# Eight of eleven chunks of a down-projection as Strassen's seven products, with the residual kept in HBM

## The chip, the core and the metric

The kernel runs on one core of one Trainium2 chip. The metric is the time of one execution on the device in microseconds (us), as the median of several runs.

## What is computed

One decoder layer for 512 prompt tokens and 8 sample tokens: norm, a mixed attention and recurrence block, an output projection with its residual, and a convolutional feed-forward block with its residual, all in float32. The change touches the end of it:

```python
D_MODEL, D_FF, CONV_W = 2048, 5632, 3
def conv_ffn(h, w_up, conv_w, conv_b, w_down, prefix):
    u = jnp.matmul(h, w_up)                      # 520 tokens x 11264
    ...                                          # causal depthwise convolution of width 3
    gate, val = jnp.split(c, 2, axis=-1)
    y = jnp.matmul(jax.nn.gelu(gate) * val, w_down)   # 520 x 5632 times 5632 x 2048
    return y, up[:, -(CONV_W - 1):]
...
x = x + jnp.matmul(mix, w_out)
y, conv_new = conv_ffn(rms_norm(x, norm2), w_up, conv_w, conv_b, w_down, conv_buf)
x = x + y                                        # then the final rmsnorm
```

## The kernel before

Activations lie transposed, features on the 128 partitions and all 520 tokens along the free axis; a matmul takes one half of them, 260 columns. To keep float32 precision each operand is split into a high part (hi, written by ACT) and the rest (lo, one subtraction on DVE). A product is then three matmuls: hi with hi, hi with lo, lo with hi. A matmul on unsplit float32 operands is one instruction ("raw" below), and takes longer.

The feed-forward part has 44 inner tiles of 128 for each of gate and value, in 11 chunks of four. Three stages follow each other on TensorE: the last part of W_out, the up-projection, the down-projection.

- **Up-projection.** It is cut into 44 "pairs", two output tiles each, numbered 0 to 43. Pair 0 is done as it is: eight raw units of eight matmuls (`first_units`), while ACT and DVE prepare the operands of the others. Pairs 1 to 43 are done by Strassen's method (`up_units`): the weights as 2 x 2 blocks (output tile n, inner parity i), the activations as 2 x 2 blocks B (inner parity, token half). Seven units take the place of eight, with the operands t1 to t4, b11, b21 and b22, made once from B and kept split, two "slots" of SBUF each. In the order in which they run, the units are 1 (b11), 4 (t4), 5 (t1), 6 (t2), 7 (t3), 2 (b21), 3 (b22). The weight sums s1 to s3 of the next pair and s2's second form (`sum1` to `sum4`) are four DVE operations a pair. The partial results leave PSUM through q1, q2 and q3 into u; unit 3 adds onto the PSUM bank from which c22 has read. In pairs 1 and 2, b11 is not split yet, and unit 1 is raw. `prep_b11` splits it in place in pair 2: ACT writes b11h, DVE the difference b11x into spare tiles, ACT b11l.
- **Convolution.** When a pair is done, a generator (`conv`) works through the convolution one step per unit, beside the next pair; at each second pair POOL stores the gated result to HBM (`ad`).
- **Down-projection.** `plain` goes over five groups of two chunks and the last chunk: eight inner tiles (four at the end) for two output tiles at a time, each product as three matmuls on two token halves. The chunks' activations come back from `ad` and are split (a0 to a10). The residual x2, which was stored to HBM (`x2d`) at the start of the up-projection, is loaded whole, 4 MB, and stays in SBUF; every result is added to it.

The code is recorded in the order in which it is written out: `units` is one list of units, and the loop at the end issues, for unit k, the weight split of unit k+2 (`prod`), its `pre` functions, its matmuls, its `post` function, and one `step` of each generator. Each engine works through its own queue in that order. Weights are loaded by SP (`load_r`, three tiles of 1 MB), activations by POOL.

```python
def split(view):
    hi = wp.tile([P, nk, P], F32R, tag="hi", name="hi", bufs=3)
    S.activation(hi, view, AF.Copy)
    lo = wp.tile([P, nk, P], F32R, tag="lo", name="lo", bufs=3)
    V.tensor_tensor(lo, view, hi.bitcast(F32), op=ALU.subtract)
```

Of the kernel before, what the change touches and what calls it, by code (L numbers as in the profile page):

```python
# [17 lines left out]
P = 128  # L18
# [50 lines left out]
def hybrid_step(ctx: ExitStack, tc: tile.TileContext, I: dict, C: dict, O: dict):  # L69
# [952 lines left out]

    xop, B = {}, {}
    R, SS, GT, UC = {}, {}, {}, {}
    pairs = [(c, o, part) for c in range(NCH) for o in (0, 2) for part in range(2)]

    def load_pair(p, n):
        c, o, part = pairs[p]  # L1030
# [21 lines left out]
    def conv(p, u):  # L1052
        c, o, part = pairs[p]
        n0 = 44 * part + 4 * c + o
        if c not in UC:
            UC[c] = fwork([P, 2, 10, 4], "uc", 2)
        G.tensor_copy(UC[c][:, part, :, o:o + 2].rearrange("p r j -> p j r"), u[:, :, T:UW])
        cv = cvtile()
        G.tensor_copy(cv[:, :, T:TT], spre[:, n0:n0 + 2])
        for j in range(2):  # L1060
            n = slice(n0 + j, n0 + j + 1)
            S.activation(cv[:, j, 0:T], u[:, j, 0:T], AF.Identity, scale=convc[:, 0, n], bias=convc[:, 3, n])  # L1062
        yield
        for j in range(2):
            n = slice(n0 + j, n0 + j + 1)
            for i, w in ((1, T), (2, TT)):
                V.scalar_tensor_tensor(cv[:, j, 0:w], u[:, j, i:i + w], convc[:, i, n], cv[:, j, 0:w],  # L1067
                                       op0=ALU.mult, op1=ALU.add)
# [5 lines left out]
        V.tensor_tensor(cv, GT[c, o], cv, op=ALU.mult)  # L1074
        nc.gpsimd.dma_start(ad[c][:, o:o + 2], cv)
# [14 lines left out]
        next(g)  # L1090
        bg.append(g)

    def first_units():

        bank, uu = {}, []

        def unit(i, n, t):
            def mm(un):
                if i == 0:
                    bank[n, t] = bankp(2 - 2 * n + t)  # L1100
                ps = bank[n, t][:, 0:HALF]
                for m in range(8):
                    PE.matmul(ps, A(0, n, i)[:, m], xg[i][t][:, m], start=i == 0 and m == 0,
                              stop=i == 1 and m == 7, skip_group_check=True)
                if i == 1:
                    if not uu:
                        uu.append(utile())
                        G.memset(uu[0][:, :, 0:2], 0.0)
                    V.tensor_tensor(uu[0][:, n, 2 + HALF * t:2 + HALF * (t + 1)], ps,
                                    rbc1[:, HALF * t:HALF * (t + 1)], op=ALU.mult)  # L1110

            return Unit(None, mm, (lambda: start_conv(0, uu[0])) if (i, n, t) == (1, 0, 1) else None)

        return [unit(i, n, t) for n in (1, 0) for i in range(2) for t in range(2)]

    def up_units(p):
        first = p == 1
        bank, st, uu = {}, {}, []

        def u():  # L1120
            if not uu:
                uu.append(utile())
                G.memset(uu[0][:, :, 0:2], 0.0)
            return uu[0]

        def out(j, t):
            return u()[:, j, 2 + HALF * t:2 + HALF * (t + 1)]
# [32 lines left out]
        def post6():  # L1160
            add("q2", "q1", 2)

        def c21():
            V.tensor_tensor(out(1, 0), st["q3"], ps(4), op=ALU.subtract)

        def c22():
            V.tensor_tensor(out(1, 1), st["q3"], ps(3), op=ALU.add)

        def post7():
            add("q3", "q2", 0)  # L1170
            c22()
            if not first:
                c21()

        def post2():
            S.copy(out(0, 0), ps(1))
# [78 lines left out]
    def prep0():  # L1255
        drain()
        for i in range(2):
            for t in range(2):
                nc.gpsimd.dma_start(x2d.rearrange("p (m i) c -> p i m c", i=2)[:, i, :, HALF * t:HALF * (t + 1)],
                                    x2b[i][t])  # L1260

    def prep_t1():
        norm2()
# [16 lines left out]
        diff(B["t"], B["t"], B[2, 1])  # L1280
        xop["t4"] = split_act(B["t"], 9, 12, "t4")

    def prep_b11():

        hi = slot(3, "b11h")
        S.activation(hi, B[1, 1], AF.Copy)
        halves = []
        for a in (0, 4):
            h = ff.tile([P, 4, HALF], F32R, tag="cv", name="b11x", bufs=3)
            V.tensor_tensor(h, B[1, 1][:, a:a + 4], hi[:, a:a + 4].bitcast(F32), op=ALU.subtract)  # L1290
            halves.append(h)
        lo = slot(13, "b11l")
        for a, h in zip((0, 4), halves):
            S.activation(lo[:, a:a + 4], h.bitcast(F32), AF.Copy)
        xop["b11"] = hi, lo
# [53 lines left out]
    ngroup = (NCH + 1) // 2  # L1349
# [172 lines left out]
```

## Time and profile before

| | us |
|---|---|
| median of 3 runs | 2321.49 (2321.19 to 2324.48) |
| the profiled execution's own time | 2320.68 |
| its span, first to last instruction | 2318.9 |
| TensorE busy / VectorE / ScalarE / GpSimd | 2277.2 / 1458.5 / 903.3 / 184.4 |
| up-projection, pairs 0 to 43 | 858 to 1781 |
| down-projection, chunks 0 to 7 | 1781 to 2150 |
| down-projection, chunks 8 to 10, final norm | 2150 to 2319 |

PE is TensorE's matmuls, PEld its weight loads, DVE VectorE, ACT ScalarE, POOL GpSimd, SP the engine that issues the weight loads. In the slices of the span a digit is the busy share in tenths; a busy PE is not a PE at its peak, since matmuls are pipelined. PEclk is the clock granted to TensorE. In a line's row stand the number of instructions, their busy time and mean, and behind the bar the idle time ahead of them with what ended it. In the timeline a row is start, duration, engine, line, operation, and in square brackets the idle time ahead of it with its releaser.

### The profile page before, as it was taken

What the parts mean: (1) busy time and instruction counts of PE and PEld (TensorE: products, weight loads), DVE (VectorE), ACT (ScalarE), POOL (GpSimd) and SP (SyncE); (2) the same over time, 40 slices, a digit from 0 to 9 for tenths busy, and PEclk for the clock granted to TensorE, in tenths of its full rate; (3) what the DMA queues carried; (4) which work ended last, traced back from release to release, by engine and by line L of the source; (5) the groups of instructions that cost most, each with busy time, mean ns of one, the idle gap of its engine ahead of it and who ended that gap; (6) DMA issues with size and microseconds to landing.
All of it is one profiled execution on the core that took longest, in us unless ns stands there. A gap on an engine that the chain in (4) does not pass through costs nothing.

```text
span 2318.9 us, 43111 instructions
## 1 busy us (share of the span) xinstructions
PE 2277.2 (98%) x18580; PEld 2254.3 (97%) x18580; DVE 1458.5 (63%) x2005; ACT 903.3 (39%) x1287; POOL 184.4 (8%) x396
## 2 busy tenths in 40 slices
PE   8999999999999998899999999999999999999996
PEld 8999999999999997899999999999999999999996
DVE  4365655444543448888889888888987433434346
ACT  6233332323342344445444445444454221222225
POOL 0001021121010120000000000000001000000002
PEclk9999999999999999999999999999999999999998
DMA  5322233234241443244434333443345533323214
GB/s 185 103 83 94 78 106 95 92 110 133 74 164 56 150 147 91 83 128 120 126 107 125 120 110 120 119 129 113 117 120 208 196 110 110 128 92 110 92 55 138
DMA packets 313357, 268.73 MB, mean 116 GB/s; under 512 B 8492, under 2 KB 299144, under 8 KB 311072
## 3 DMA queue, kind: packets, MB, share of 16 engines
q1 hardware_dynamic: 298608, 212.56, 29.7%
q0 software_dynamic: 14560, 53.43, 6.6%
q8 instruction: 146, 2.39, 0.4%
q14 instruction: 43, 0.35, 0.0%
HBM read 240.25 MB, written 28.12 MB: 116 GB/s over the span
## 4 chain that ended last, share of the span: by engine, by line
PE 72%; DVE 3%; ACT 1%; issue 1%; DMA 0%; ACTq 0%; DVEq 0%; POOLq 0%
PE pw L967 25%; PE pw L1142 12%; PE pw L1141 12%; PE pw L1140 12%; PE pg L186 3%; PE pg L190 3%; PE pg L188 3%; DVE lo L931 1%; PE psc L703 1%; PE pob L685 1%; DVE n L1239 0%; ACT hi L929 0%; PE px L750 0%; DVE x L1347 0%; PE ppt L693 0%
## 5 line engine op out<-in xcount | busy, mean ns | idle before, releaser
L929 ACT ACTIVATE hi<-r 128x1024 fp32r<-128x1024 f32 (+1 forms) x248 | 250.7, 1015 | 504.6 <-PE pw L967 363.4
L931 DVE TENSOR_TENSOR lo<-r,hi 128x1024 fp32r<-128x1024 f32 (+1 forms) x248 | 298.6, 1205 | 54.2 <-ACT hi L929 54.2
L186 PE MATMUL pg<-x1h,hi 128*128 128x260 f32 x1408 | 290.0, 287 | 3.0 <-ACT hi L157 1.7
L190 PE MATMUL pg<-x1h,lo 128*128 128x260 f32 x1408 | 284.3, 284 | 0.5 <-DVE lo L159 0.5
L188 PE MATMUL pg<-x1l,hi 128*128 128x260 f32 x1408 | 283.4, 283 | 0.0
L1347 DVE TENSOR_TENSOR x<-pw,x 128x260 f32<-128x260 f32 (+2 forms) x192 | 74.0, 423 | 267.1 <-PE pw L967 263.4
L931 DVE TENSOR_TENSOR lo<-s,hi 128x1024 fp32r<-128x1024 f32 x171 | 209.1, 1223 | 44.1 <-ACT hi L929 40.2
L159 DVE TENSOR_TENSOR lo<-raw,hi 128x1024 fp32r<-128x1024 f32 x104 | 127.2, 1223 | 168.5 <-ACT hi L157 162.2
L929 ACT ACTIVATE hi<-s 128x1024 fp32r<-128x1024 f32 x171 | 180.6, 1057 | 113.1 <-PE pw L1141 103.3
L186 PEld LDWEIGHTS pg<-x1h,hi 128*128 128x128 f32 x1408 | 217.8, 189 | 4.3 <-ACT hi L157 2.0
L190 PEld LDWEIGHTS pg<-x1h,lo 128*128 128x128 f32 x1408 | 217.4, 189 | 0.7 <-DVE lo L159 0.7
L188 PEld LDWEIGHTS pg<-x1l,hi 128*128 128x128 f32 x1408 | 217.2, 189 | 0.0
L1067 DVE SCALAR_TENSOR_TENSOR cv<-u,convc,cv 128x512 f32<-128x512 f32 (+1 forms) x176 | 132.2, 751 | 43.8 <-ACT cv L1062 43.8
L157 ACT ACTIVATE hi<-raw 128x1024 fp32r<-128x1024 f32 x104 | 109.6, 1055 | 43.1 <-PE pg L188 36.6
L1062 ACT ACTIVATE cv<-u,convc 128x512 f32<-128x512 f32 x88 | 67.0, 809 | 98.0 <-DVE u L1183 93.6
L1140 PE MATMUL pw<-t1h,hi 128*128 128x260 f32 x344 | 98.7, 287 | 2.4 <-ACT hi L929 2.4
L1140 PE MATMUL pw<-t3h,hi 128*128 128x260 f32 x344 | 98.5, 286 | 2.3 <-ACT hi L929 2.3
L1142 PE MATMUL pw<-t3h,lo 128*128 128x260 f32 x344 | 98.4, 286 | 0.8 <-DVE lo L931 0.8
L1142 PE MATMUL pw<-t1h,lo 128*128 128x260 f32 x344 | 98.0, 285 | 0.8 <-DVE lo L931 0.8
L1140 PE MATMUL pw<-t4h,hi 128*128 128x260 f32 x344 | 97.9, 285 | 0.0
L1141 PE MATMUL pw<-t3l,hi 128*128 128x260 f32 x344 | 97.9, 285 | 0.0
L1142 PE MATMUL pw<-t2h,lo 128*128 128x260 f32 x344 | 97.3, 283 | 0.6 <-DVE lo L931 0.6
(487 smaller groups left out, 6451.4 us busy)
## 6 DMA issues: line engine op xcount, KB each, us to landing
r<-in_w_up SPq DMA_DIRECT2D x88, 1024.0 KB, 5.4
raw<-in_w_in SPq DMA_DIRECT2D x88, 512.0 KB, 3.6
r<-in_w_down SPq DMA_DIRECT2D x40, 1024.0 KB, 5.2
ad<-cv POOLq DMA_DIRECT2D x22, 520.0 KB, 3.5
a<-ad POOLq DMA_DIRECT2D x11, 1040.0 KB, 5.3
raw<-in_w_out SPq DMA_DIRECT2D x16, 512.0 KB, 3.3
r<-in_w_out SPq DMA_DIRECT2D x8, 1024.0 KB, 5.2
r<-in_w_down SPq DMA_DIRECT2D x13, 512.0 KB, 3.3
```

What stands on the lines that cost most here:

```text
L157: S.activation(hi, raw, AF.Copy)
L159: V.tensor_tensor(lo, raw, hi.bitcast(F32), op=ALU.subtract)
L186: PE.matmul(ps[:, i, 0:b - a], wh, xh[:, a:b], start=first, stop=False)
L188: PE.matmul(ps[:, i, 0:b - a], wh, xl[:, a:b], start=False, stop=False)
L190: PE.matmul(ps[:, i, 0:b - a], wl, xh[:, a:b], start=False, stop=last)
L929: S.activation(hi, view, AF.Copy)
L931: V.tensor_tensor(lo, view, hi.bitcast(F32), op=ALU.subtract)
L967: PE.matmul(ps[t][:, 0:b - a], wt[:, kk], x[:, a:b], start=kk == 0 and wt is hi and x is xh, stop=kk == nk - 1 and wt is lo)
L1067: V.scalar_tensor_tensor(cv[:, j, 0:w], u[:, j, i:i + w], convc[:, i, n], cv[:, j, 0:w], op0=ALU.mult, op1=ALU.add)
L1140: PE.matmul(ps(k), hi[:, m], xh[:, m], start=a, stop=False, skip_group_check=True)
L1141: PE.matmul(ps(k), hi[:, m], xl[:, m], start=False, stop=False, skip_group_check=True)
L1142: PE.matmul(ps(k), lo[:, m], xh[:, m], start=False, stop=z, skip_group_check=True)
```

## The change

The first eight chunks of the down-projection are done by the same seven products. `pairs` gets 16 more entries, numbered 44 to 59: two groups of 16 inner tiles (chunks 0 to 3, and 4 to 7), with eight pairs of output tiles each. The first pair of a group (44 and 52) is done as it is, in raw matmuls; in the next two, unit 1 is raw; the other five have all seven products split. `first_units` and `up_units` become `as_is_units` and `seven_units`, and a sink (`Up` or `Down`) says where results go. `Down` adds into a tile of the residual in place: the pair's two output tiles are loaded from HBM by POOL one pair ahead (`load_xs`) and stored back behind the pair. `x2d` is cut into four tensors, and its first stores go over SP in 16 pieces instead of over POOL in four. The gated activations of a group lie in one tensor (`agd`), and its four blocks B are loaded from there in the pair ahead of the group, into slots that the old operands leave. `b11` of a group is split in the group's third pair ahead of its fourth unit (`U2[3]`); in the up-projection that stands ahead of the sixth (`U2[5]`), as before. Chunks 8 to 10 keep the plain form.

```diff
+    NWG = 2
+    agd = [dram.tile([P, KT, TT], F32, name=f"agd{g}") for g in range(NWG)]
...
+    NUP = len(pairs)
+    pairs += [(g, n0) for g in range(NWG) for n0 in range(0, KT, 2)]
+    as_is = [0] + [NUP + KT // 2 * g for g in range(NWG)]
...
+    class Down:
+        def add(self, n, t, v, op=ALU.add):
+            x = xs_of[self.p][:, n, HALF * t:HALF * (t + 1)]
+            V.tensor_tensor(x, x, v, op=op)
+        def whole(self, n, t, ps):
+            self.add(n, t, ps)
+        def c11(self, ps):
+            self.add(0, 0, ps)
+        def c12(self, q2, ps):
+            self.add(0, 1, q2)
+            self.add(0, 1, ps)
+        def c21(self, q3, ps):
+            self.add(1, 0, q3)
+            self.add(1, 0, ps, ALU.subtract)
+        def c22(self, q3, ps):
+            self.add(1, 1, q3)
+            self.add(1, 1, ps)
+        def done(self):
+            n0 = pairs[self.p][1]
+            nc.gpsimd.dma_start(x2d[n0 // 4][:, n0 % 4:n0 % 4 + 2], xs_of[self.p])
+
+    def load_xs(p):
+        if NUP <= p < len(pairs):
+            n0 = pairs[p][1]
+            xs_of[p] = cvtile()
+            nc.gpsimd.dma_start(xs_of[p], x2d[n0 // 4][:, n0 % 4:n0 % 4 + 2])
...
         def post7():
             add("q3", "q2", 0)
-            c22()
+            out.c22(st["q3"], ps(3))
             if not first:
-                c21()
+                out.c21(st["q3"], ps(4))
...
-        if p < 3:
+        if p - 1 in as_is or p - 2 in as_is:
             U[1] = Unit(None, mm_raw(1, lambda: A(p, 0, 0), (1, 1), True), post1)
...
+        at[6].pre.append(lambda: load_xs(p + 1))
...
     def prep0():
...
-                nc.gpsimd.dma_start(x2d.rearrange("p (m i) c -> p i m c", i=2)[:, i, :, HALF * t:HALF * (t + 1)],
-                                    x2b[i][t])
+                for q in range(4):
+                    nc.sync.dma_start(
+                        x2d[q].rearrange("p (m i) c -> p i m c", i=2)[:, i, :, HALF * t:HALF * (t + 1)],
+                        x2b[i][t][:, 2 * q:2 * q + 2])
...
-    U2[5].pre.append(prep_b11)
+    U2[5].pre.append(lambda: prep_b11(3, 13, "cv", 3))
...
+    def group(g, old):
+        f = [i for k in ORDER for i in old[k]]
+        new = {"t1": (f[5], f[6]), "t2": (f[7], f[8]), "t3": (f[10], f[11]), "t4": (f[12], f[13]),
+               "b21": (f[1], f[9]), "b22": (f[3], f[4]), "b11": (f[2], f[0])}
+        p = NUP + KT // 2 * g
+        prev, N, U1, U2 = ups[p - 1:p + 3]
...
+        def t2():
+            diff(B["t"], B[2, 2], B["t"])
+            cut("t2")
...
+        prev[1].pre += [lambda: load_b(1, 1, f[0]), lambda: load_b(1, 2, f[1])]
+        prev[2].pre += [lambda: load_b(2, 2, f[2]), lambda: load_b(2, 1, f[3])]
+        N[0].pre.append(t1)
+        N[2].pre.append(t2)
+        N[4].pre.append(t3)
+        N[5].pre.append(t4)
+        N[6].pre += [lambda: sum1(p + 1), lambda: sum3(p + 1)]
+        N[7].pre.append(lambda: sum2(p + 1))
+        U1[0].pre.append(lambda: split_b(2, 1, "b21", *new["b21"]))
+        U1[1].pre.append(lambda: split_b(2, 2, "b22", *new["b22"]))
+        U2[3].pre.append(lambda: prep_b11(*new["b11"], "u", 2))
+        return new
...
-    dl = [(8 * g, 8, n0) for g in range(ngroup - 1) for n0 in range(0, KT, 2)]
+    dl = [(4 * C0 + 8 * g, 8, n0) for g in range(ngroup - 1) for n0 in range(0, KT, 2)]
```

What this does to the queues is shown at three places. First ACT where b11 is split; n and g are B's blocks, hi the high part of a weight block r or a weight sum s. Before, in pair 2 (the only such place):

```order
L929 ACTIVATE hi<-r_9298 128x1024
L929 ACTIVATE hi<-s_9497 128x1024
L929 ACTIVATE hi<-r_9499 128x1024
L1286 ACTIVATE b11h<-n_9189 128x2080
L1294 ACTIVATE b11l<-b11x 128x1040 x2
L1176 COPY u<-pw_9509 128x260
L929 ACTIVATE hi<-r_9501 128x1024
```

Now, in pair 46, the third of the first new group (pair 54 is alike):

```order
L935 ACTIVATE hi<-s_19701 128x1024
L935 ACTIVATE hi<-r_19578 128x1024
L1361 ACTIVATE b11h<-g_19248 128x2080
L1369 ACTIVATE b11l<-b11x 128x1040 x2
L935 ACTIVATE hi<-s_19734 128x1024
L935 ACTIVATE hi<-r_19798 128x1024
```

In pair 2 all the pair's own weight blocks are split ahead of b11, and the copy of c11 stands behind it; in pair 46 the split of s2 for the pair's last unit stands behind it.

Second DVE, at the same two pairs; q is the sum of partial results, pw a PSUM bank, lo the low part of a weight. Before:

```order
L931 TENSOR_TENSOR lo<-s_9497,hi 128x1024
L1044 TENSOR_TENSOR s_9621<-r_9499,r_9501 128x1024
L1154 TENSOR_TENSOR q_9648<-q_9613,pw_9623 128x260
L1167 TENSOR_TENSOR u<-q_9648,pw_9556 128x260
L1164 TENSOR_TENSOR u<-q_9648,pw_9525 128x260
L931 TENSOR_TENSOR lo<-r_9499,hi 128x1024
L1047 TENSOR_TENSOR s_9658<-s_9586,r_9499 128x1024
L1290 TENSOR_TENSOR b11x<-n_9189,b11h 128x1040 x2
```

Now:

```order
L1056 TENSOR_TENSOR s_19876<-r_19800 128x1024
L1365 TENSOR_TENSOR b11x<-g_19248,b11h 128x1040 x2
L1231 TENSOR_TENSOR q_19912<-q_19811,pw_19887 128x260
L937 TENSOR_TENSOR lo<-s_19734,hi 128x1024
L1059 TENSOR_TENSOR s_19918<-r_19798,r_19800 128x1024
L1231 TENSOR_TENSOR q_19945<-q_19912,pw_19920 128x260
L1145 TENSOR_TENSOR cv<-cv,q_19945 128x260
L1145 TENSOR_TENSOR cv<-cv,pw_19847 128x260
```

b11x moves from behind c22 and c21 (L1167, L1164) to ahead of q2 and q3, and c22 is two additions into the residual tile cv instead of one into u.

Third POOL, at the end of the up-projection. Before:

```order
L1324 DMA a_19239<-ad_8104 128x2080
L1324 DMA a_19241<-ad_8105 128x2080
L1123 MEMSET u 128x2x2
L1057 COPY uc<-u 128x2x10
L1059 COPY cv<-spre 128x2x8
L1343 DMA x_19451<-x2d 128x2080
```

Now:

```order
L1408 DMA g_19248<-agd_8107 128x8x260
L1408 DMA g_19250<-agd_8107 128x8x260
L1408 DMA g_19283<-agd_8107 128x8x260
L1408 DMA g_19285<-agd_8107 128x8x260
L1116 MEMSET u 128x2x2
L1173 DMA cv<-x2d_8103 128x1040
```

The loads of a chunk (a) give way to the four blocks of the first group (g), and the load of a quarter of the residual (x) to that of one pair's two tiles (cv).

More of the change, by code (lines that the diff above doesn't have):

```diff
@@ L870, in hybrid_step, with a_rows @@
     spre = ffc.tile([P, 88, NB], F32, name="spre")
-    x2d = dram.tile([P, KT, TT], F32, name="x2d")
-    ad = [dram.tile([P, 4, TT], F32, name=f"ad{c}") for c in range(NCH)]
+    x2d = [dram.tile([P, 4, TT], F32, name=f"x2d{q}") for q in range(4)]
+    NWG = 2
+    agd = [dram.tile([P, KT, TT], F32, name=f"agd{g}") for g in range(NWG)]
+    acd = {c: dram.tile([P, 4, TT], F32, name=f"acd{c}") for c in range(4 * NWG, NCH)}
+    def a_rows(c):
+        return acd[c] if c >= 4 * NWG else agd[c // 4][:, 4 * (c % 4):4 * (c % 4) + 4]
     def fwork(shape, tag, bufs=1):
@@ L1074, in conv @@
         V.tensor_tensor(cv, GT[c, o], cv, op=ALU.mult)
[L1075 removed]
+        nc.gpsimd.dma_start(a_rows(c)[:, o:o + 2], cv)
         if o == 2:
@@ L1091, in start_conv, with __init__, at, whole @@
         bg.append(g)
-    def first_units():
-        bank, uu = {}, []
+    class Up:
+        def __init__(self, p):
+            self.p, self.uu = p, []
+        def at(self, j, t):
+            if not self.uu:
+                self.uu.append(utile())
+                G.memset(self.uu[0][:, :, 0:2], 0.0)
+            return self.uu[0][:, j, 2 + HALF * t:2 + HALF * (t + 1)]
+        def whole(self, n, t, ps):
+            V.tensor_tensor(self.at(n, t), ps, rbc1[:, HALF * t:HALF * (t + 1)], op=ALU.mult)
+        def c11(self, ps):
+            S.copy(self.at(0, 0), ps)
+        def c12(self, q2, ps):
+            V.tensor_tensor(self.at(0, 1), q2, ps, op=ALU.add)
+        def c21(self, q3, ps):
+            V.tensor_tensor(self.at(1, 0), q3, ps, op=ALU.subtract)
+        def c22(self, q3, ps):
+            V.tensor_tensor(self.at(1, 1), q3, ps, op=ALU.add)
+        def done(self):
+            start_conv(self.p, self.uu[0])
+    xs_of = {}
+    class Down:
+        def __init__(self, p):
+            self.p = p
+        def add(self, n, t, v, op=ALU.add):
+            x = xs_of[self.p][:, n, HALF * t:HALF * (t + 1)]
+            V.tensor_tensor(x, x, v, op=op)
+        def whole(self, n, t, ps):
+            self.add(n, t, ps)
+        def c11(self, ps):
+            self.add(0, 0, ps)
+        def c12(self, q2, ps):
+            self.add(0, 1, q2)
+            self.add(0, 1, ps)
+        def c21(self, q3, ps):
+            self.add(1, 0, q3)
+            self.add(1, 0, ps, ALU.subtract)
+        def c22(self, q3, ps):
+            self.add(1, 1, q3)
+            self.add(1, 1, ps)
+        def done(self):
+            n0 = pairs[self.p][1]
[5 more added lines that the diff above has]
+            nc.gpsimd.dma_start(xs_of[p], x2d[n0 // 4][:, n0 % 4:n0 % 4 + 2])
+    def sink_of(p):
+        return Up(p) if p < NUP else Down(p)
+    def as_is_units(p):
+        bank, out = {}, sink_of(p)
         def unit(i, n, t):
@@ L1101, in mm, with seven_units @@
                 ps = bank[n, t][:, 0:HALF]
+                x = xg[i][t] if p == 0 else B[i + 1, t + 1]
                 for m in range(8):
-                    PE.matmul(ps, A(0, n, i)[:, m], xg[i][t][:, m], start=i == 0 and m == 0,
+                    PE.matmul(ps, A(p, n, i)[:, m], x[:, m], start=i == 0 and m == 0,
                               stop=i == 1 and m == 7, skip_group_check=True)
                 if i == 1:
[L1106 to L1116, printed above, removed]
-        first = p == 1
[L1118 to L1127, printed above, removed]
+                    out.whole(n, t, ps)
+            return Unit(None, mm, out.done if (i, n, t) == (1, 0, 1) else None)
+        at = [unit(i, n, t) for n in (1, 0) for i in range(2) for t in range(2)]
+        at[0].pre.append(lambda: load_pair(p + 1, 0))
+        at[4].pre.append(lambda: load_pair(p + 1, 1))
+        at[7].pre.append(lambda: load_xs(p + 1))
+        return at
+    def seven_units(p):
+        first = p == 1
+        bank, st, out = {}, {}, sink_of(p)
         def ps(k):
@@ L1212, in up_units @@
                 at[0].pre.append(lambda: load_pair(nx, 1))
+            if not first and nx not in as_is:
                 at[3].pre.append(lambda: sum1(nx))
@@ L1215, in up_units @@
                 at[5].pre.append(lambda: sum2(nx))
+        at[6].pre.append(lambda: load_xs(p + 1))
         return at
-    ups = [first_units()] + [up_units(p) for p in range(1, len(pairs))]
+    ups = [as_is_units(p) if p in as_is else seven_units(p) for p in range(len(pairs))]
     for at in ups:
@@ L1318, in hybrid_step @@
+    for g in range(NWG):
+        places = group(g, places)
     x2 = [None] * 4
     a_raw, a_hl = {}, {}
-    SETS = (((9, 12), (1, 2)), ((4, 5), (6, 7)))
+    free = [i for k in ORDER for i in places[k]]
+    C0 = 4 * NWG
+    SETS = ((free[2:4], free[4:6]), (free[6:8], free[12:14]))
     def load_a(c):
-        a_raw[c] = bigt((3, 13)[c % 2], f"a{c}", F32)
-        nc.gpsimd.dma_start(a_raw[c], ad[c])
+        a_raw[c] = bigt(free[c % 2], f"a{c}", F32)
+        nc.gpsimd.dma_start(a_raw[c], a_rows(c))
@@ L1326, in split_a @@
     def split_a(c):
-        h, l = SETS[c // 2 % 2][c % 2]
+        h, l = SETS[(c - C0) // 2 % 2][c % 2]
         a_hl[c] = split_act(a_raw[c], h, l, f"a{c}", 4, (P, 4, TT))
     def next_a(g):
-        for c in range(2 * g, min(2 * g + 2, NCH)):
+        some = range(C0 + 2 * g, min(C0 + 2 * g + 2, NCH))
+        for c in some:
             load_a(c)
@@ L1335, in next_a @@
             yield
-        for c in range(2 * g, min(2 * g + 2, NCH)):
+        for c in some:
             split_a(c)
```

66 lines of the change are left out of this document (43 added, 23 removed).

## The prediction

> **What bounds the kernel now.** I read the page first: engines, slices, chain that ended last.
>
> ```profile
> span 2318.9 us, 43111 instructions
> PE 2277.2 (98%) x18580; PEld 2254.3 (97%) x18580; DVE 1458.5 (63%) x2005; ACT 903.3 (39%) x1287; POOL 184.4 (8%) x396
> ...
> PE   8999999999999998899999999999999999999996
> ...
> DVE  4365655444543448888889888888987433434346
> ...
> PEclk9999999999999999999999999999999999999998
> ...
> PE 72%; DVE 3%; ACT 1%; issue 1%; DMA 0%; ACTq 0%; DVEq 0%; POOLq 0%
> ```
>
> TensorE is busy almost everywhere and most of the chain is its own. So time goes down only if it issues less, and each us in which it waits is added. VectorE is at 80 to 90% in the up-projection (slices 15 to 30), where Strassen runs already, and at 30 to 40% in the down-projection. The change carries the first pattern into the second place. Next the table by stages (columns: busy us and count of PE, PEld, DVE, ACT, POOL; granted clock; DMA share; GB/s), and when the matmuls of chunks 0 and 8 and of the as-is pair start.
>
> ```profile
> 950.40:1740.90 790.50, 790.47 (x6562) 790.47 (x6563) 698.02 (x800) 386.04 (x460) 49.30 (x176) 1.00 0.39 118
> ...
> 1781.20:1873.40 92.20, 92.20 (x771) 92.20 (x770) 41.30 (x58) 22.41 (x23) 7.33 (x15) 1.00 0.54 197
> ```
>
> ```profile
> L967 PE MATMUL pw<-a0h,hi x128: 278/282/366, 1781.3 to 1870.0; 128*128 128x260 f32 x128
> ...
> L967 PE MATMUL pw<-a8h,hi x128: 278/282/292, 2149.9 to 2238.5; 128*128 128x260 f32 x128
> ...
> L1103 PE MATMUL pw<-xg,r x128: 380/382/383, 858.4 to 888.0; 128*128 128x260 f32 x128
> ```
>
> 39 Strassen pairs with all seven products split fill 790.5 us without a gap. Chunks 0 to 7 of the down-projection take 2149.9 - 1781.3 = 368.6 us, 0.120 us for each of 3072 matmuls. The as-is pair's 64 unsplit matmuls stand in 128 records, 29.6 us from first start to last: 0.466 us each.
>
> **How a group of pairs begins.** The only place that shows it is the up-projection's start, pairs 0 to 2, in the timeline: TensorE's four longest waits there, then the queue ahead of the longest, then the clock about them.
>
> ```profile
> 899.93 0.39 PE L1140 MATMUL pw<-t3h,hi 128*128 128x260 f32 x1 [2.28 <-ACT hi L929]
> ...
> 926.22 0.39 PE L1140 MATMUL pw<-t1h,hi 128*128 128x260 f32 x1 [2.43 <-ACT hi L929]
> ...
> 943.24 0.36 PE L1140 MATMUL pw<-b22h,hi 128*128 128x260 f32 x1 [1.83 <-DVE u L1167]
> ...
> 950.43 0.58 PE L1140 MATMUL pw<-b11h,hi 128*128 128x260 f32 x1 [4.06 <-ACT u L1176]
> ```
>
> ```profile
> 939.45 1.93 ACT L1286 ACTIVATE b11h<-n 128x2080 fp32r<-128x2080 f32 x1
> ...
> 945.62 2.38 DVE L1290 TENSOR_TENSOR b11x<-n,b11h 128x1040 fp32r<-128x1040 f32 x2
> 948.09 2.03 ACT L1294 ACTIVATE b11l<-b11x 128x1040 fp32r<-128x1040 f32 x2 [6.71 <-issue]
> 950.02 0.36 ACT L1176 COPY u<-pw 128x260 f32<-128x260 f32 x1
> ```
>
> ```profile
> 900.50:907.30 6.80, 6.11 (x25) 5.92 (x26) 6.80 (x7) 1.93 (x2) 0.00 (x0) 0.50 0.01 2
> ...
> 948.30:955.10 6.80, 4.67 (x21) 4.67 (x22) 2.31 (x3) 5.03 (x7) 0.37 (x3) 0.50 0.18 49
> ```
>
> The b11 operand is split in place: ACT writes b11h, DVE the difference, ACT b11l. ACT stands still in between, and what is queued behind b11l is late: here a copy of 0.36 us for which TensorE waited 4.06 us. After such waits the granted clock falls to 0.50: of the 6.8 us from 948.3, TensorE worked 4.67 at half speed, a further 2.3 us lost.
>
> **The sum.** (1) Matmul work removed: 368.6 us. (2) Work put in, for a group of eight pairs. As-is pair: 64 x 0.466 = 29.8 us, against 192 x 0.120 = 23.0 in the plain form, so this pair loses 6.8. A split matmul in Strassen's order: (790.5 - 2.3 at half clock) / (39 x 168) = 0.1203 us. The two pairs with raw b11: 144 x 0.1203 + 8 x 0.466 = 21.05 each. Five full pairs: 168 x 0.1203 = 20.2 each. Group: 29.8 + 42.1 + 101.0 = 172.9; two groups 345.8. Removed less added: 22.8 us gained, if nothing waits.
>
> (3) DVE's cover. Its pieces:
>
> ```profile
> L931 DVE TENSOR_TENSOR lo<-s,hi 128x1024 fp32r<-128x1024 f32 x40 | 48.9, 1223 | 10.0 <-ACT hi L929 9.0
> L929 ACT ACTIVATE hi<-s 128x1024 fp32r<-128x1024 f32 x40 | 42.3, 1057 | 26.0 <-PE pw L1141 26.0
> ...
> L1041 DVE TENSOR_TENSOR s<-r 128x1024 f32<-128x1024 f32 x10 | 12.2, 1218 | 0.0
> ...
> L1154 DVE TENSOR_TENSOR q<-q,pw 128x260 f32<-128x260 f32 x20 | 8.4, 418 | 0.0
> ```
>
> ```profile
> 872.51 2.38 DVE L1253 TENSOR_TENSOR t<-n,n 128x1040 f32<-128x1040 f32 x2
> 874.88 2.40 DVE L1248 TENSOR_TENSOR t1l<-t,t1h 128x1040 fp32r<-128x1040 f32 x2
> ...
> 1753.50 1.23 DVE L1074 TENSOR_TENSOR cv<-cv 128x1040 f32<-128x1040 f32 x1
> ```
>
> ```profile
> L1067 DVE SCALAR_TENSOR_TENSOR cv<-u,convc,cv 128x512 f32<-128x512 f32 (+1 forms) x176 | 132.2, 751 | 43.8 <-ACT cv L1062 43.8
> ```
>
> A steady Down pair: 7 splits and 4 sums at 1.22, q2, q3 and seven in-place adds at 0.42 = 17.2 us, under TensorE's 20.2; the up pairs ran at 698/790 = 88% without a gap. Zero. The as-is pair: four differences and four splits, 4 x 4.78 = 19.1, three sums 3.7, four adds 1.7, and for group 0 the rest of pair 43's convolution, 4 x 0.75 and the product of 1.23: 28.7 against 29.8. The pair behind it: six splits 7.3, b21 and b22 4.8, sums 4.9, adds 3.8 = 20.8 against 21.05. Also covered, but with hardly 1 us to spare. This is the thinnest cover of the sum; if it is gone, that is the slower rival below. The differences' operands are loads now, of 1040 KB each.
>
> (4) b11, the term that I do not hide. Its split now stands before pair 46's fourth unit (54 in group 1). Counted from that pair's start, with the durations above: its third unit ends at 3.7 + 2 x 2.89 = 9.5, which frees a hi buffer; hi 1.06 (10.6), on DVE lo 1.22 and sum1 1.22 (13.0), with b11h 1.93 beside them; b11x 2.38 (15.4); b11l 2.03 (17.4). Queued behind b11l is the hi for the pair's last unit: 1.06 (18.5), lo 1.22 (19.7), sum3 (20.9), q3 0.42, and c22, which is now two adds (22.2). The last unit adds onto the bank that c22 reads, and is due at 3.7 + 5 x 2.89 = 18.2. TensorE waits 4.0 us. Bounds: 0 if the order of arrival hides it, 4.06 + 1.83 = 5.9 if both waits of pair 2 return. I take 4.0, nearest to the 4.06 that this split cost before. The clock then costs between 0 and half of 6.8 = 3.4; I take the 2.3 of that place. 6.3 a group, 12.6 for both.
>
> [...]
>
> (5) DMA and queues.
>
> ```profile
> r<-in_w_down SPq DMA_DIRECT2D x40, 1024.0 KB, 5.2
> ad<-cv POOLq DMA_DIRECT2D x22, 520.0 KB, 3.5
> ...
> x2d<-x POOLq DMA_DIRECT2D x4, 1040.0 KB, 8.2
> x<-x2d POOLq DMA_DIRECT2D x4, 1040.0 KB, 13.0
> ```
>
> ```profile
> 860.89 0.85 POOL L1259 DMA_DIRECT2D x2d<-x  x1 [0.85 <-issue]
> ...
> 874.36 0.37 SPq L923 DMA_DIRECT2D r<-in_w_up  x1
> ...
> 884.85 1.22 DVE L1041 TENSOR_TENSOR s<-r 128x1024 f32<-128x1024 f32 x1
> ```
>
> The four B loads of a group are issued from pair 43's second and third unit on (about 3 to 7 us into it) and first used 20 to 28 us into it; at 13 us they land in time. A pair's residual load is issued a pair ahead and read 14 us into its own pair. Its store waits for the last add on POOL, but nothing due stands behind it except the next such load. At 3.5 to 13 us both are hidden by the pair's 20 us. The x2d stores move from POOL to SP as 16 pieces in front of the load of 874.36. They wait for the last W_out evacuations, as POOL's last issue at 860.89 did. 13 us lie between, and 16 issues at 0.37 to 0.87 take 6 to 14, so at worst that load is 1 us late, and its first reader starts at 884.85. Zero. At the end, the last x2 load waits for the last store, 3.5 us, while its first reader is six pairs away. Zero.
>
> Sum: -22.8 + 12.6 = -10.2 us on the profiled execution's 2320.7 (span 2318.9 and 1.8 around it): 2310.5. The runs' median is 0.8 above it: 2311.3, so 2311.5.
>
> **Rivals.** A, the forecast: two b11 stalls with the clock's dip, 2306 to 2316. B: b11 is hidden, with no wait and no dip: 2321.5 - 22.8 = 2298.7. For it: ACT works 386 of 790 us in the up stage, and splits are issued two units, 5.8 us, ahead. Against it: the 6.71 us of ACT behind this very split. C, no change: in a steady Down pair, c22 is later than in an up pair.
>
> ```profile
> 1740.93 0.28 PE L1140 MATMUL pw<-b11h,hi 128*128 128x260 f32 x1
> ...
> 1756.93 0.42 DVE L1154 TENSOR_TENSOR q<-q,pw 128x260 f32<-128x260 f32 x1
> 1757.38 0.42 DVE L1167 TENSOR_TENSOR u<-q,pw 128x260 f32<-128x260 f32 x1
> ```
>
> This pair's fifth unit ends at 1740.93 + 5 x 2.88 = 1755.3, c22 at 1757.8, and the last unit is due at 1758.2. One add more makes that 1758.2: no slack. If DVE runs as late here, each further us on 14 pairs costs 14 us; at 0.7 us a pair the gain is gone (2321.5). Against it: no convolution and no product in the pair, which is 3 us less on DVE. D, slower: a group begins as badly as the up-projection did, because DVE's thin cover in the as-is pair breaks and each split then comes late. There, 858.4 to 950.4 is 92.0 us. Its matmuls are 29.8, 22.7 (pair 1: three products raw, 3 x 3.73 + 4 x 2.89) and 21.05, together 73.6: 18.4 us lost. Twice that is 36.8 - 22.8 = +14.0, so 2335.5. It decides from 11.4 us a group on. Against it: the up start also had eight normalisation operations on DVE, 9.4 us by the row of the first four, and the norm itself to wait for.
>
> ```profile
> 867.90 4.69 DVE L1239 TENSOR_TENSOR n<-xg,rbc 128x1040 f32<-128x1040 f32 x4
> ```
>
> **How the numbers follow.** A measurement of this kernel tells about 0.2% (4.6 us) from no change: 2316.8 and 2326.1 are the bounds. A 0.66, B 0.12, C with mixtures of stalls 0.12, D 0.10. Faster: A, B and a little of C, 0.79; same 0.11; slower 0.10. The range leaves D out: from B's 2298 to 2322.
>
> **What the profile after would show.** Matmul records fewer by the terms of (2); pairs 47 to 51 at 20.2 us from t4 to t4; as-is pairs 29.8. For A: one wait of about 4 us at a b22 matmul in each group, put down to DVE's c22 add, and granted clock 0.5 for 3.4 to 6.8 us there. For B no such wait; for C short waits at b22 in every pair; for D waits at t1 to t4 in the pair behind the as-is pair. I am wrong if the waits named in D appear, or if a residual load is what DVE waits for.

## The result, and the profile after

The changed kernel takes 2307.98 us (median of 4 runs, 2307.24 to 2309.51) against 2321.72 (4 runs): a ratio of 0.9939, 95% interval 0.9922 to 0.9957, so 13.7 us less. The forecast was 2311.5 in 2298 to 2322. The profiled execution's span went from 2318.9 to 2305.2, also 13.7. The page of the changed kernel, the lines that answer to those shown of before:

```profile
span 2305.2 us, 42433 instructions
PE 2255.0 (98%) x18084; PEld 2221.7 (96%) x18084; DVE 1591.7 (69%) x2125; ACT 955.0 (41%) x1345; POOL 200.9 (9%) x424
...
DVE  4365655444553448888888888988887977877446
...
PE 71%; DVE 4%; ACT 1%; issue 1%; DMA 0%; ACTq 0%; DVEq 0%; POOLq 0%
```

TensorE has 22 us less to do and is still the bound. VectorE now stands at 70 to 90% in chunks 0 to 7 of the down-projection too (slices 32 to 37). When the first new raw matmul and the first of chunk 8 start (duration min, median and max in ns, then first and last start):

```profile
L1189 PE MATMUL pw<-g,r x256: 380/382/385, 1780.7 to 1984.7; 128*128 128x260 f32 x128
...
L973 PE MATMUL pw<-a8h,hi x128: 278/282/387, 2134.5 to 2224.8; 128*128 128x260 f32 x128
```

Chunks 0 to 7 take 2134.5 - 1780.7 = 353.8 us, against 368.6: 14.8 less. They begin 0.6 earlier, and what follows takes 170.7 instead of 169.0. So -14.8 - 0.6 + 1.7 = -13.7. The windows of the two groups, and of pairs 47 to 51 within the first:

```profile
1854.60:1956.00 101.40, 101.40 (x842) 101.40 (x842) 77.69 (x98) 36.38 (x38) 8.90 (x14) 0.99 0.57 184
1780.70:1956.80 176.10, 172.18 (x1291) 167.25 (x1290) 142.51 (x169) 69.29 (x72) 14.76 (x26) 0.99 0.52 166
1956.80:2134.80 178.00, 173.81 (x1291) 168.58 (x1290) 142.88 (x167) 73.53 (x76) 9.04 (x17) 0.98 0.49 159
```

The five full pairs run without a gap, 20.3 us each. In the 176.1 us of the first group TensorE stands still for 3.92, in the 178.0 of the second for 4.2. TensorE's timeline shows these waits, and a new one at chunk 8:

```profile
1851.65 0.36 PE L1217 MATMUL pw<-b22h,hi 128*128 128x260 f32 x1 [3.92 <-DVE cv L1145]
...
2027.75 0.56 PE L1217 MATMUL pw<-b22h,hi 128*128 128x260 f32 x1 [3.92 <-DVE cv L1145]
...
2131.53 0.36 PE L1217 MATMUL pw<-b22h,hi 128*128 128x260 f32 x1 [0.24 <-ACT a9h L1320]
...
2136.02 0.39 PE L973 MATMUL pw<-a8h,hi 128*128 128x260 f32 x1 [1.25 <-DVE cv L1145]
```

The two long waits stand where the prediction put them, in pairs 46 and 54, at b22, behind the c22 add (L1145; c11, c12, c21 and c22 are a pair's four results, by output tile and token half). What stands ahead of the first, on ACT and then on DVE:

```profile
1839.98 1.93 ACT L1361 ACTIVATE b11h<-g 128x2080 fp32r<-128x2080 f32 x1
1844.87 2.04 ACT L1369 ACTIVATE b11l<-b11x 128x1040 fp32r<-128x1040 f32 x2 [2.96 <-DVE b11x L1365]
1846.82 1.04 ACT L935 ACTIVATE hi<-s 128x1024 fp32r<-128x1024 f32 x1
```

```profile
1842.39 2.39 DVE L1365 TENSOR_TENSOR b11x<-g,b11h 128x1040 fp32r<-128x1040 f32 x2
...
1847.89 1.23 DVE L937 TENSOR_TENSOR lo<-s,hi 128x1024 fp32r<-128x1024 f32 x1 [2.78 <-ACT hi L935]
...
1851.08 0.42 DVE L1145 TENSOR_TENSOR cv<-cv,pw 128x260 f32<-128x260 f32 x1
```

ACT is free from 1841.9 but stands for 2.96 us at b11l, which needs b11x; the hi of s2 is queued behind b11l; DVE stands for 2.78 us at the lo of s2; sum3, q3 and the two adds of c22 follow, and TensorE starts 0.15 us after the second.

### The profile page after: what moved, and what is told of

Same layout as the page of the kernel before. It is cut to its first block, busy times and chain, and to the rows that moved or that the text cites. A ratio compares the mean times of both kernels' runs of the same rounds, so it can differ in the third digit from the quotient of the medians.

```text
span 2305.2 us, 42433 instructions
## 1 busy us (share of the span) xinstructions
PE 2255.0 (98%) x18084; PEld 2221.7 (96%) x18084; DVE 1591.7 (69%) x2125; ACT 955.0 (41%) x1345; POOL 200.9 (9%) x424
## 4 chain that ended last, share of the span: by engine, by line
PE 71%; DVE 4%; ACT 1%; issue 1%; DMA 0%; ACTq 0%; DVEq 0%; POOLq 0%
PE pw L1218 16%; PE pw L1217 16%; PE pw L1219 16%; PE pw L973 9%; PE pg L186 3%; PE pg L190 3%; PE pg L188 3%; PE pw L1189 3%; DVE lo L937 1%; PE pw L1225 1%; ACT hi L935 1%; PE psc L703 1%; PE pob L685 1%; DVE n L1312 0%; PE px L750 0%
## 5 line engine op out<-in xcount | busy, mean ns | idle before, releaser
L937 DVE TENSOR_TENSOR lo<-s,hi 128x1024 fp32r<-128x1024 f32 x227 | 277.7, 1223 | 91.8 <-ACT hi L935 88.1
L935 ACT ACTIVATE hi<-s 128x1024 fp32r<-128x1024 f32 x227 | 240.0, 1058 | 187.0 <-PE pw L1218 174.4
L1217 PE MATMUL pw<-b22h,hi 128*128 128x260 f32 x448 | 129.1, 288 | 9.9 <-DVE cv L1145 7.8
L1219 PE MATMUL pw<-t3h,lo 128*128 128x260 f32 x456 | 130.1, 285 | 0.6 <-DVE lo L937 0.6
L1219 PE MATMUL pw<-t1h,lo 128*128 128x260 f32 x456 | 129.8, 285 | 0.7 <-DVE lo L937 0.7
L1217 PE MATMUL pw<-t4h,hi 128*128 128x260 f32 x456 | 130.3, 286 | 0.0
L1218 PE MATMUL pw<-t3l,hi 128*128 128x260 f32 x456 | 129.7, 284 | 0.0
L1219 PE MATMUL pw<-t4h,lo 128*128 128x260 f32 x456 | 129.1, 283 | 0.5 <-DVE lo L937 0.5
L1219 PE MATMUL pw<-t2h,lo 128*128 128x260 f32 x456 | 128.9, 283 | 0.6 <-DVE lo L937 0.6
L1218 PE MATMUL pw<-t1l,hi 128*128 128x260 f32 x456 | 129.4, 284 | 0.0
```

What stands on the lines that cost most here:

```text
L1217: PE.matmul(ps(k), hi[:, m], xh[:, m], start=a, stop=False, skip_group_check=True)
L1218: PE.matmul(ps(k), hi[:, m], xl[:, m], start=False, stop=False, skip_group_check=True)
L1219: PE.matmul(ps(k), lo[:, m], xh[:, m], start=False, stop=z, skip_group_check=True)
```

## The experiments

Where no range is given, the time is that of one run; the changed kernel's four runs lie within 2.3 us of each other, and the medians of the kernel before, measured again beside the experiments, lie between 2320.2 and 2321.7. A dip is a stretch at half the granted clock. The way out is the step from a group's last pair to the plain form.

**The wait behind b11l.** Theory: the two waits and their clock dips come only from what is queued behind b11l on ACT. Three versions take `prep_b11` of the groups apart or move it. First, one part per unit: b11h, b11x and b11l ahead of the second, third and fourth unit.

```diff
-        U2[3].pre.append(lambda: prep_b11(*new["b11"], "u", 2))
+        U2[1].pre.append(lambda: b11_high(new["b11"][0]))
+        U2[2].pre.append(lambda: b11_rest("u", 2))
+        U2[3].pre.append(lambda: b11_low(new["b11"][1]))
```

> The split of b11 in the new groups is taken apart: b11h ahead of the third pair's second unit, b11x ahead of its third, b11l ahead of its fourth, instead of all three ahead of the fourth. Theory Q (what is queued behind b11l on ACT is late): both waits of 3.92 us at b22 and both dips of the clock (3.4 and 6.9 us at half) are gone, 7.8 + 4.6 = 12.4 us, so about 2295.6 us. Rival R (DVE is late by itself, since c22 became two in-place adds): the b22 waits stay at 2 us or more each and the time stays above 2303.

Measured: 2300.69 us (2299.27 to 2301.81), ratio 0.9910 (0.9895 to 0.9924), so 7 us below the change. Its timeline of TensorE in pair 46 and 47:

```profile
1850.72 0.36 PE L1217 MATMUL pw<-b22h,hi 128*128 128x260 f32 x1 [1.34 <-DVE cv L1145]
...
1854.13 0.36 PE L1217 MATMUL pw<-b11h,hi 128*128 128x260 f32 x1 [0.30 <-DVE cv L1145]
```

The 3.92 became 1.34 + 0.30, in both groups alike, and the granted clock stays at 1.00 there. The groups went from 353.8 to 345.5 us. It misses the expected 2295.6 for two reasons. First, 1.6 us a group stay; b11x (2.39 us) still stands on DVE ahead of c22, which fits, but no run takes it away from there without moving other work. Second, the groups begin 1.7 us later than in the profile of the change, at 1782.4, before anything that was edited: the up-projection began 0.8 later (859.2 against 858.4), and the half clock behind its own b11 wait lasted 5.3 us instead of 3.4.

Second, only b11l one unit later, so that the hi of s2 stands ahead of it.

```diff
-        U2[3].pre.append(lambda: prep_b11(*new["b11"], "u", 2))
+        U2[3].pre.append(lambda: b11_high(new["b11"][0]))
+        U2[3].pre.append(lambda: b11_rest("u", 2))
+        U2[4].pre.append(lambda: b11_low(new["b11"][1]))
```

> b11h and b11x stay ahead of the fourth unit, only b11l moves to ahead of the fifth, behind the hi of s2. Theory Q: that hi starts at about 12.3 us into the pair instead of 17, and DVE gets to c22 1 us after b22 is due: b22 waits 1.0 us in each group, no dip, about 2298. Rival P (it is the place of b11x on DVE, ahead of q2 and q3, that makes c22 late): b22 still waits 3 us or more.

Measured: 2300.09 us. TensorE's timeline, then the window about it:

```profile
1849.71 0.36 PE L1217 MATMUL pw<-b22h,hi 128*128 128x260 f32 x1 [1.06 <-ACT hi L935]
...
1853.12 0.36 PE L1217 MATMUL pw<-b11h,hi 128*128 128x260 f32 x1 [0.29 <-DVE cv L1145]
```

```profile
1846.00:1856.00 10.00, 8.64 (x71) 8.29 (x70) 9.79 (x15) 4.78 (x5) 0.69 (x2) 1.00 0.18 51
```

1.06 us of wait where 1.0 was expected, granted clock 1.00, groups of 344.9 us. The expected 2298 is missed by 2: the groups begin 0.9 later than in the change, and what follows them takes 1.0 more. Only the place of b11l among ACT's instructions was changed, b11h and b11x stand as before: so the queue behind b11l is shown to be the cause of 2.6 of the 3.92 us and of both dips.

Third, the whole `prep_b11` ahead of the sixth unit (`U2[5]` for `U2[3]`), where the up-projection has it.

> The whole split of b11 ahead of the sixth unit, U2[5], where the up-projection has it. Theory Q: nothing of this pair stands behind b11l any more, so no wait at b22; but b11l itself ends about 3.5 us after the next pair's first matmul is due, so the wait moves to b11 in pairs 47 and 55: 3 to 4 us each and a dip, and the time is that of the change within 3 us. Rival R: waits at b22 and at b11, 5 us slower.

Measured: 2304.79 us, 3.2 below the change. The wait moved to the b11 matmuls of the next pair and was shorter than expected, 2.3 us in each group; most of it is put down to DVE's add of a result, which stands behind b11x, and only the rest to b11l:

```profile
1854.82 0.37 PE L1217 MATMUL pw<-b11h,hi 128*128 128x260 f32 x1 [1.88 <-DVE cv L1145]
1855.56 0.58 PE L1218 MATMUL pw<-b11l,hi 128*128 128x260 f32 x1 [0.37 <-ACT b11l L1369]
```

**One group instead of two** (`NWG = 1`; chunks 4 to 7 plain again).

> One group instead of two: chunks 0 to 3 as Strassen's products, chunks 4 to 10 in the plain form. If the gain is the groups' own, the first one keeps its part, 184.3 us of plain work against 176.0, less 1.3 at the way out: 2322 - 7.0 - 0.6 = 2314.4. Rival: what is gained or lost lies in what the change does once (residual in four tensors, stores on SP, the way out): then it stays near 2308 or goes to 2322.

Measured: 2317.60 us (2315.48 to 2319.04, 10 runs), ratio 0.9984 (0.9975 to 0.9994). TensorE's timeline at the group's wait and its way out:

```profile
1852.82 0.36 PE L1217 MATMUL pw<-b22h,hi 128*128 128x260 f32 x1 [3.92 <-DVE cv L1145]
...
1960.00 0.39 PE L973 MATMUL pw<-a4h,hi 128*128 128x260 f32 x1 [1.24 <-DVE cv L1145]
```

The group runs from 1781.9 to 1958.5, 176.6 us against 184.4 in plain form: 7.8 gained, where 8.3 was expected. But the span fell by only 3.4, and the time is 3.2 above the expected 2314.4. Chunks 4 to 7, plain, took 186.2 instead of 184.2, of which 1.24 is the wait shown, the last stretch 170.8 instead of 169.0, and the group began 0.6 later. So leaving the seven-product form has a price, a wait of about 1.25 us (1.24 here, 1.25 at chunk 8 in the change), that the first group of two does not pay. Of the 1.8 us at the end, where no such wait stands in this kernel, 1.0 lies behind chunks 8 and 9, in chunk 10 and the final norm. The rest (a8's hi matmuls take 89.4 us from first start to last, 88.6 in the kernel before), and what chunks 4 to 7 lost besides the wait, is spread over the matmuls with no wait to show for it. The cause of all of this is open.

**How thin VectorE's cover is.** The third difference of the as-is pair is computed three times (its halves take 6.99 us of DVE instead of 2.39):

```diff
-            diff(t, B[2, 2], B[1, 2])
+            for _ in range(3):
+                diff(t, B[2, 2], B[1, 2])
```

> t3's difference is computed three times instead of once in each as-is pair: 4.8 us more on VectorE (two more of 2 x 1.2). If the cover of the as-is pair and the pair behind it is as thin as the trace of the change shows (VectorE without a gap for 45 us, 0.3 us to spare at the b22 matmuls of pair 45), group 0 loses 4 to 4.8 us at pair 45 in waits behind VectorE, with a half-clock window possible (0 to 3 us more); group 1, which has no convolution beside it and so about 4.5 us more to spare, loses under 0.5 us. Time 2312 to 2316. Rival: VectorE has several us to spare in both groups, nothing waits, time as the change, 2308.

Measured: 2316.28 us, 8.3 above the change and just above the range. TensorE's timeline in pairs 45 and 53:

```profile
1816.09 0.39 PE L1219 MATMUL pw<-t4h,lo 128*128 128x260 f32 x1 [1.50 <-DVE lo L937]
1825.67 0.39 PE L1219 MATMUL pw<-t3h,lo 128*128 128x260 f32 x1 [0.37 <-DVE lo L937]
1833.03 0.36 PE L1217 MATMUL pw<-b22h,hi 128*128 128x260 f32 x1 [1.57 <-DVE cv L1145]
...
1995.61 0.39 PE L1219 MATMUL pw<-t4h,lo 128*128 128x260 f32 x1 [0.58 <-DVE lo L937]
2005.18 0.39 PE L1219 MATMUL pw<-t3h,lo 128*128 128x260 f32 x1 [0.37 <-DVE lo L937]
2012.55 0.36 PE L1217 MATMUL pw<-b22h,hi 128*128 128x260 f32 x1 [1.59 <-DVE cv L1145]
```

3.4 us in group 0, at t4, t3 and b22; 2.5 us in group 1, where under 0.5 was expected. So both groups are thin. Group 1 has no convolution beside it, and in the change DVE is busy for 23.94 of the 28.1 us of its as-is pair, against 26.81 in group 0, but the room cannot be used, as DVE's timeline of the change itself shows:

```profile
1971.09 0.43 DVE L1145 TENSOR_TENSOR cv<-cv,pw 128x260 f32<-128x260 f32 x1 [3.08 <-PE pw L1189]
1971.43 2.39 DVE L1326 TENSOR_TENSOR t<-g,g 128x1040 f32<-128x1040 f32 x2
```

DVE worked in its queue's order here: the difference for t3 stands behind an add that waits 3.08 us for TensorE. Between the two profiles the span differs by 9.1 us. Of these, 6.0 are the waits shown; another 1.8 stand ahead of the groups, which begin at 1782.5 here. That the time came so near the range is partly luck: group 1's waits and the late start stand in for what group 0 did not lose.

**The residual through HBM.** Load and store of each pair are left out (zero fill by POOL; one store in each group stays), and so the output lacks the down-projection of chunks 0 to 7.

```diff
-            nc.gpsimd.dma_start(xs_of[p], x2d[n0 // 4][:, n0 % 4:n0 % 4 + 2])
+            G.memset(xs_of[p], 0.0)
...
-            nc.gpsimd.dma_start(x2d[n0 // 4][:, n0 % 4:n0 % 4 + 2], xs_of[self.p])
+            if pairs[self.p][1] == 0:
+                nc.gpsimd.dma_start(x2d[0][:, 0:2], xs_of[self.p])
```

> The residual's load and store per pair of the seven-product stretch are left out (a zero fill by GpSimd in their place, one store kept), so the down-projection's result of chunks 0 to 7 is left out of the output. If the transfers are hidden, as the prediction had it: within 1.5 us of the change, and the same waits at b22, 3.9 us each. Rival: the transfers cost something by contention with the weight loads or by late residual tiles: 3 us or more faster.

Measured: 2308.40 us (2305.04 to 2309.09), ratio 0.9942 (0.9925 to 0.9958), where the change has 0.9939; the waits at b22 are 3.98 and 3.99. The groups take 176.4 and 177.7 us, where the change has 176.1 and 177.6. The transfers cost nothing that can be measured.

**The up-projection's own b11, and the way out.** Both versions have b11l one unit later in the groups, split a8 and a9 one unit earlier at the way out, and take the up-projection's b11 apart. The late one:

```diff
-    U2[5].pre.append(lambda: prep_b11(3, 13, "cv", 3))
+    U2[4].pre.append(lambda: b11_high(3))
+    U2[4].pre.append(lambda: b11_rest("cv", 3))
+    U2[5].pre.append(lambda: b11_low(13))
...
-    last[4].pre += [lambda: split_a(C0), lambda: load_d(2)]
-    last[5].pre.append(lambda: split_a(C0 + 1))
+    last[3].pre.append(lambda: split_a(C0))
+    last[4].pre += [lambda: split_a(C0 + 1), lambda: load_d(2)]
```

> As the version whose b11l stands one unit later in each new group; besides, the way out splits a8 and a9 one unit earlier, and in the up-projection b11h and b11x stand ahead of the fifth unit of pair 2 and b11l ahead of the sixth (all three ahead of the sixth before). Theory: the 2.8 to 4.1 us at the first b11 matmul of pair 3 come from c11's copy behind b11l, as in the new groups; with b11l a unit earlier the wait and its clock dip go, 4 to 6 us, and the way out gives 1.0 to 1.5: 2293 to 2296. Rival: VectorE is without a gap there from 926 to 948 us, so b11x ahead of other work only moves the wait to another operand: 2298 to 2301.

The early one has `b11_high` at `U2[3]`.

> As the one before, with b11h ahead of the fourth unit of pair 2, b11x ahead of the fifth and b11l ahead of the sixth. Theory: same as the one before within 1 us, 2293 to 2296, since ACT is idle where b11h goes. Rival: 2298 to 2301.

Measured: 2300.02 and 2300.55 us, within the rival's range, but not for its reason alone. TensorE's timeline of the late one:

```profile
946.19 0.38 PE L1217 MATMUL pw<-b22h,hi 128*128 128x260 f32 x1 [4.16 <-DVE u L1132]
...
2123.92 0.49 PE L1217 MATMUL pw<-b22h,hi 128*128 128x260 f32 x1 [2.88 <-DVE cv L1145]
```

In pair 2, two waits (1.85 and 4.09 in the version with only b11l later) became one of 4.16: a gain of 2.7 us (922.9 to 920.2) by the distance from the up-projection's start to the groups'. At the way out, both splits (2.39 us each) now stood on DVE ahead of c22: a wait of 2.88 us and 3.4 us at a granted clock of 0.50 took the gain back. So the last version leaves a8's split where the change has it and puts a9's behind c11's add:

```diff
-    last[5].pre.append(lambda: split_a(C0 + 1))
+    last[6].pre.append(lambda: split_a(C0 + 1))
```

> b11l one unit later in each new group, the up-projection's b11 apart as in the late version of the two before, and at the way out only a9's split moved, behind c11's add (a8's stays where the change has it). Theory: the up start keeps its gain of about 2.5 us, the way out loses its 1.25 us wait and gets no new one, the groups keep 1.06 and 0.3 us each: 2300 less 2.5 and less 1.2, 2296 to 2297. Rival: a9's low part now comes too late for the first plain unit, and the wait only moves there: 2298 or more.

Measured: 2296.29 us (2295.62 to 2296.72), ratio 0.9894 (0.9878 to 0.9911), as expected. The way out keeps 0.24 us of wait:

```profile
2121.46 0.36 PE L1217 MATMUL pw<-b22h,hi 128*128 128x260 f32 x1 [0.24 <-DVE cv L1145]
```

This beats both kernels: 11.7 us below the change, or 10.4 by the two ratios, each taken against the kernel before as measured beside it, and 1.1% below the kernel before.

## Why the prediction was right, point by point

- **Work removed, 368.6:** as said; it is read from before. The matmul records fell from 18580 to 18084, and the 496 fewer are what the terms of (2) give: 1288 in a group instead of 1536.
- **Work put in, two groups of 172.9, mis-sized.** Without waits the groups measure 172.18 and 173.81, less the half-clock losses of 1.7 and 2.9 (below): 170.5 and 170.9, together 4.4 below the 345.8. The step that was off is 0.466 us for a raw matmul. It came from pair 0's 29.6 us as if nothing else had run there. The groups of lines within that stretch, of before, and of the changed kernel's pair 44:

```profile
L1103 PE MATMUL pw<-xg,r 128*128 128x260 f32 x128 | 28.4, 382 | 0.0
L1229 PE MATMUL ms<-u,onesD 128*128 128x260 f32 x8 | 1.9, 382 | 0.0
```

```profile
L1189 PE MATMUL pw<-g,r 128*128 128x260 f32 x128 | 28.3, 382 | 0.0
```

  Pair 0 also held 8 records of the norm's sums, 1.9 us. The price is 28.3 / 64 = 0.44 us. That is 1.6 us for each as-is pair and 0.2 for each of the four pairs with a raw unit, 4.0 of the 4.4. Pair 44 itself takes 28.2 us instead of 29.8. The rows stood in the profile of before.
- **DVE's cover, zero with hardly 1 us to spare:** confirmed. In pair 45 of the changed kernel c22's second add ends 0.29 us before TensorE's b22 begins:

```profile
1826.08 0.42 DVE L1145 TENSOR_TENSOR cv<-cv,pw 128x260 f32<-128x260 f32 x1
```

```profile
1826.79 0.28 PE L1217 MATMUL pw<-b22h,hi 128*128 128x260 f32 x1
```

  What the sum implied, that group 1 would be easier without the convolution, did not hold (the run with the third difference computed three times). Rival D rested on a break of this cover; 4.6 us more on DVE brought 3.4 and 2.5 of waits, still far from the 11.4 a group at which D decides.
- **b11, 4.0 us of wait and 2.3 of clock a group:** measured 3.92 twice, and 1.7 and 2.9, so 12.4 in all against 12.6. The chain ACT, DVE, c22, b22 is the one that was written down, step for step: from the start of pair 46 (1829.7) b11x ends at 15.1 us (15.4 in the prediction), b11l at 17.2 (17.4), c22 at 21.8 (22.2), and b22 was due at 18.05 (18.2). Moving b11l alone breaks it. That the clock's part came to the 2.3 a group that was taken is luck: it is the mean of 1.7 and 2.9, which two waits of equal length cost at two places on the clock's grid (last section). Rival B (no wait) is what the second experiment makes of the kernel, but for 1.35 us.
- **Rival C, c22 late in each pair:** no wait in the five full pairs of the first group; DVE is at 77.69 of 101.40.
- **DMA and queues, zero:** confirmed by the run without the residual's transfers. In neither group does DVE wait for a residual load. The weight load behind the pieces on SP is issued at 874.42 instead of 874.36, and its first reader starts at 884.91 instead of 884.85, so the pieces delay nothing; a version with the pieces back on POOL was not run.
- **The way out, zero:** wrong. c11's add, which ACT did in the up-projection, now stands on DVE behind the split of a9, and a matmul of chunk 8 waits 1.25 us for it. Only the last loads and stores were costed there. DVE's timeline of the changed kernel:

```profile
2133.24 2.39 DVE L1321 TENSOR_TENSOR a9l<-a,a9h 128x1040 fp32r<-128x1040 f32 x2
2135.54 0.42 DVE L1145 TENSOR_TENSOR cv<-cv,pw 128x260 f32<-128x260 f32 x1
```

  That is 1.25 of the 1.7 us; with a9's split behind that add, in the last version, the wait is gone.
- **Phase (where the work falls on the clock's grid):** the up-projection's wait behind its b11l, untouched by the change, ends at 950.43 in both profiles. The half clock behind it lasted to 955.1 before; now the clock is full up to 951.4 and half to 954.9. That is 4.7 against 3.4 us, and half of the difference is the 0.6 us by which the groups begin earlier. A half-clock stretch ahead of the wait, from 944.6, costs nothing now, as the wait is the shorter for it (2.79 us, 4.06 before):

```profile
950.43 0.38 PE L1217 MATMUL pw<-b11h,hi 128*128 128x260 f32 x1 [2.79 <-ACT u L1123]
```

  No reading of the diff could give that.

So the mechanism was right, and -10.2 became -13.7 by -4.6 in the groups, +1.7 behind them and -0.6 ahead.

## What to carry to other kernels

Before a price per instruction is taken from the length of a stretch, list all groups of lines within it: strangers in the stretch are charged to the instruction. Where engines take their instructions in the recorded order, as ACT and DVE did here (s2's hi stood behind a b11l that waited 2.96 us), a step that is split over two engines (ACT, DVE, ACT) should be recorded in parts, with the other work that is due put between them; here one line moved was worth 2.6 us a group and the clock besides. When a result's last step is moved to another engine, ask at the end of the stretch too what is queued ahead of it there.

## What the runs showed of the hardware

In the profiles of both kernels the changes of the granted clock, 11 before and 17 in the changed kernel, lie whole multiples of 3.41 us apart, on a grid of cells of that length. In the other nine profiles each of the 611 such cells looked at reads 1.00 or 0.50 as a whole. The cells of the changed kernel about the two long waits, and about b22 in pair 2 (behind the window and its length in us stand TensorE's busy time and count; the granted clock is the third from the end):

```profile
1849.14:1852.55 3.41, 0.90 (x7) 0.93 (x8) 3.31 (x7) 0.61 (x1) 0.00 (x0) 1.00 0.00 0
1852.56:1855.97 3.41, 3.41 (x18) 3.41 (x17) 3.41 (x5) 0.00 (x0) 0.00 (x0) 0.50 0.00 0
2023.22:2026.63 3.41, 0.60 (x6) 0.40 (x4) 2.65 (x3) 2.62 (x3) 0.00 (x0) 1.00 0.00 0
2026.64:2030.05 3.41, 2.30 (x10) 2.33 (x11) 3.31 (x7) 0.00 (x0) 0.00 (x0) 0.50 0.00 0
2030.05:2033.46 3.41, 3.41 (x17) 3.41 (x17) 2.57 (x5) 0.36 (x1) 0.00 (x0) 0.50 0.04 12
941.20:944.61 3.41, 1.56 (x13) 1.41 (x12) 3.38 (x6) 0.18 (x1) 0.10 (x1) 1.00 0.69 241
944.61:948.02 3.41, 3.03 (x15) 2.73 (x13) 3.39 (x3) 0.00 (x0) 0.00 (x0) 0.50 0.00 0
```

The same cell of the kernel before, and the one behind it:

```profile
941.47:944.88 3.41, 1.64 (x13) 1.67 (x14) 3.38 (x6) 0.00 (x0) 0.00 (x0) 1.00 0.52 197
944.88:948.29 3.41, 1.49 (x13) 1.28 (x11) 3.12 (x3) 0.20 (x1) 0.00 (x0) 1.00 0.00 0
```

The wait of 3.92 us fell on the grid so that the cell up to 1852.55 was idle for 2.51 of 3.41 us and the next one ran at half; it was busy throughout, and the clock came back: half of 3.41, an estimated 1.7 us lost. The second wait of the same length reached 1.11 us into the half-clock cell, and a second cell ran at half: (2.30 + 3.41) / 2 = 2.9 us lost. In pair 2, 1.85 us idle in a cell were followed by half clock in the changed kernel, 1.77 us idle in the same cell were not in the one before; there the clock fell one cell later. The grid lies 0.27 us earlier against the same work; no other difference of that size shows there, and the 0.6 us of phase are put down to it. The cells of all eleven profiles between 887 and 967, 1802 and 1868, 1982 and 2043, and 2107 and 2143 us, about the starts and ends of the groups and of the up-projection's first pairs, were counted in the same way, each with the cell behind it. Of 647 at full clock, 44 were followed by half clock, and these had been idle for 1.68 to 3.41 us; the 603 others had been idle for 1.80 us at most. Of 55 at half clock, 12 were followed by another, after 0.60 to 2.13 us idle; the 43 others had been idle for 0.45 us at most. This is a count, with no run made to test it, and other stretches of the same profiles need not agree: far ahead of them, the cell from 746.90 to 750.31 before and that from 746.63 to 750.04 in the changed kernel, filled by matmuls of four columns and a few of 260, have TensorE busy for 3.41 of 3.41 us at 1.00, and the next cell of each reads 0.50.

In the counted cells at full clock, then, idle time of under 1.6 us was followed by no half clock, while the change's two waits of 3.92 us cost 1.7 and 2.9 more, at two places on the grid. So a difference of a microsecond or two need not come from the edit: in the profiles whose edits touch only the groups and what follows, the first group begins anywhere from 1780.7 to 1783.1.
